# Fourteen seven-product pairs in each half of a down projection, and the group tiles of the up projection joined

## The chip, the cores and the metric

The kernel runs on one core of a Trainium2 chip. A core has a matrix engine (TensorE, PE in the profile, with its weight loads as PEld), a vector engine (VectorE, DVE), an activation engine (ScalarE, ACT), a general one (GpSimd, POOL), a queue for transfers (SyncE, SP), and 16 DMA engines that all queues share. The metric is the device time of one execution in microseconds; lower is better.

## The reference, cut to what matters

One layer of an encoder on 256 positions (`T`) of width 2048. The change lies in the last part, the channel mixer, whose middle width is 5504 (43 chunks of 128):

```python
def conv_ffn(x, g_norm, w_up, conv_k, conv_b, w_down):
    h = rms_norm(x, g_norm)
    up = h @ w_up                                    # 2048 -> 2 * 5504
    t = up.shape[1]
    pad = jnp.pad(up, ((0, 0), (1, 1), (0, 0)))
    up = (pad[:, :t] * conv_k[0] + pad[:, 1:t + 1] * conv_k[1]
          + pad[:, 2:t + 2] * conv_k[2] + conv_b)
    gate, val = jnp.split(up, 2, axis=-1)
    return x + (jax.nn.silu(gate) * val) @ w_down    # 5504 -> 2048
```

Before it stand a mixer block (`x @ w_in`, a gated branch, neighbourhood attention, two merging projections), after it a final RMS norm. All data is float32.

## The kernel before, in words

**Precision.** Each matrix operand is split into a high part (ScalarE copies it into a tile of a shorter float type) and a low part (VectorE subtracts that from the original). A block product is three matmuls: high by high, low by high, high by low (`triple`, lines 317 to 319).

**Pieces.** Weights come in pieces of 512 KB or less. `load_to` starts the load of a piece on SP's queue (line 145 or 151) into one of five tiles `wraw`; `split_to` makes its high part `whi` (ScalarE, line 170) and its low part `wlo` (VectorE, line 171), each in one of four tiles, so that a piece's part can be written once TensorE has read that of the piece four before. `begin(i)` runs at each piece `i`: it loads up to five pieces ahead, splits up to three ahead, then runs the tasks that were hung on step `i` with `at(i, f)`. The order in which the program calls the operations is the order on every engine; nothing is reordered later. So an operation that waits holds back all that stands behind it on its engine.

**Up projection** (`run_group`, `spread_products`, lines 222 and 226). There are 22 groups of eight pieces. A group makes two chunks of the gate and two of the value (the last group, chunk 42, one of each). Its products with the low weights come in one go for two pieces. When a group's products are done, `ev_up(f0, nb)` takes the results out of PSUM: a ScalarE copy (`tb`) and a VectorE sum (`ta`) for each chunk. Then, as tasks on the steps of the next group, `conv(b)` multiplies by the norm's factor (line 1067), ScalarE makes the middle tap (line 1069), VectorE adds the side taps (lines 1072 and 1074); `gate` follows one step later, and the split of the result into `ff["a"]` one more. The two chunks of a group are done in turn: `conv(0)` one step after the group, `conv(1)` three steps after it, or five for the group before the last. 256 columns each.

**Seven products instead of eight.** The down projection works in two halves of 1024 output columns, each a run of 43 pieces (one chunk of 128 rows each). For two row blocks of positions and two column blocks of 512, a pair of pieces takes 2 x 12 matmuls, or, in the places listed in `DOWN_QUADS`, 21 (Strassen's scheme in Winograd's form, `run_wide`). Such a pair needs sums of its activations and sums of its weights. The sums of activations are made once in the up projection, written to memory by POOL's queue (`ff["kept"]`, line 1094) and read back for each half (`stored`, line 1391). The sums of weights are made on VectorE from the loaded pieces (`weight_sums`, `weight_sums_split`), except for the pairs in `DOWN_SPLIT`: their sums and splits are made during the up projection by `split_ahead` (lines 1286 to 1301), written to memory, and read back as four tiles of 512 KB (`split_read`, line 1251); such a pair then loads half of its first piece. The kept tiles are single ones (`h13`, `l13`, `h24`, `l24` in the pool `twice`), the kept activation sums go round three tiles.

**Places.** Before, each half has 13 such pairs, four of them kept (6, 10, 14, 18), and the first half's first is the fourth pair. `DOWN_JOBS` names the groups of the up projection in which the jobs of `split_ahead` run, one for each kept pair and half.

Lines in the profile are those of the kernel file. The functions that the change touches:

Of the kernel before, what the change touches and what calls it, by code (L numbers as in the profile page):

```python
# [8 lines left out]
F32 = mybir.dt.float32  # L9
BF16 = mybir.dt.bfloat16  # L10
F32R = mybir.dt.float32r
AF = mybir.ActivationFunctionType
# [4 lines left out]
T = 256  # L17
# [50 lines left out]
TURN_X2 = (13, 1)  # L68
Y_GAP = 224
PAD = 16  # L70
DOWN_PAIRS = (3, 5, 6, 7, 9, 10, 11, 13, 14, 15, 17, 18, 19)
DOWN_QUADS = (DOWN_PAIRS, (2, 4, 5, 6, 8, 9, 10, 12, 13, 14, 16, 17, 18))
DOWN_SPLIT = (6, 10, 14, 18)
DOWN_JOBS = ((1, 3), (5, 7), (9, 11), (13, 17))
FIN_AT = 36


# [1 line left out]
def trunk_kernel(ctx, tc, x, x_t, vecs, w_in, ln_g, ln_b, w_st, b_s, rpb, w_branch, w_out, w_up, w_down,  # L79
# [4 lines left out]
    def pool(name, side="left", bufs=1, space=None):  # L84
        kw = {} if space is None else {"space": space}
        st = ExitStack()
        p = st.enter_context(tc.tile_pool(name=name, bufs=bufs, side=side, reuse_waits="tile", **kw))
        return p, st
# [100 lines left out]
    def at(i, f):  # L189
        tasks.setdefault(i, []).append(f)  # L190
# [130 lines left out]
    def act_blocks(w, a11, a21, a12, a22):  # L321
        s3, n1, p2, s4 = (w[:, n * 128:(n + 1) * 128] for n in range(4))
        nc.vector.tensor_sub(s3, a11, a21)
        nc.vector.tensor_sub(n1, a22, a21)
        nc.vector.tensor_add(p2, n1, a11)
        nc.vector.tensor_sub(s4, a12, p2)
# [213 lines left out]
    def split_plain(p, dst):  # L540
        nc.scalar.activation(dst[:, 0, :], p, AF.Copy)
        nc.vector.tensor_sub(dst[:, 1, :], p, dst[:, 0, :].bitcast(F32))
# [508 lines left out]

    def ev_up(f0, nb):
        def done(ps, i):
            n = nb
            a = []
            own = {}
            for p in ps:
                t = turns["p"].tile([128, T], F32, name="tb", bufs=3)
                nc.scalar.activation(t, p[:, T:], AF.Copy)
                u = turns["p"].tile([128, T], F32, name="ta", bufs=6)  # L1060
                nc.vector.tensor_add(u, p[:, :T], t)
                a.append(u)

            def conv(b):
                c = []
                for u, ch in ((a[b], f0 + b), (a[n + b], NF + f0 + b)):
                    nc.vector.tensor_mul(u, u, rs["rb"])  # L1067
                    v = ff["p"].tile([128, T], F32, name="tc", bufs=4)
                    nc.scalar.activation(v, u, AF.Identity, scale=ck[:, 1, ch:ch + 1], bias=ck[:, 3, ch:ch + 1])  # L1069
                    c.append((u, v, ch))  # L1070
                for u, v, ch in c:
                    nc.vector.scalar_tensor_tensor(v[:, 1:], u[:, :T - 1], ck[:, 0, ch:ch + 1], v[:, 1:],  # L1072
                                                   op0=OP.mult, op1=OP.add)
                    nc.vector.scalar_tensor_tensor(v[:, :T - 1], u[:, 1:], ck[:, 2, ch:ch + 1], v[:, :T - 1],
                                                   op0=OP.mult, op1=OP.add)
                at(cur[0] + 1, lambda: gate(b, c[0][1], c[1][1]))

            def gate(b, g, v):
                nc.scalar.activation(g, g, AF.Silu)
                nc.vector.tensor_mul(g, g, v)  # L1080
                at(cur[0] + 1, lambda: split_plain(g, ff["a"][f0 + b]))
                own[b] = g
                if b and f0 // 2 in ff["kept"]:
                    at(cur[0] + 2, sums)
                    at(cur[0] + 3, sums_split)

            def sums():
                own["w"] = ff["more"].tile([128, 512], F32, name="sw")
                act_blocks(own["w"], *(own[k][:, t * 128:(t + 1) * 128] for k in range(2) for t in range(2)))

            def sums_split():
                o = ff["more"].tile([128, 2, 512], F32R, name="so")
                split_plain(own["w"], o)
                nc.gpsimd.dma_start(ff["kept"][f0 // 2], o.bitcast(F32))

            at(i + 1, lambda: conv(0))
            if n > 1:
                at(i + (5 if f0 + 3 == NF else 3), lambda: conv(1))
        return done


# [297 lines left out]
    def down_order(g):  # L1399
# [4 lines left out]

    g_dn = [wide(w_d, 0, down_order(g), g * 1024, lambda k: ff["a"][k], DOWN_QUADS[g], down_room,
                 (ev_sums(2 * g, down_room), ev_down if g == 0 else finish), stored=stored,
                 split=({p: (6, 6) for p in DOWN_SPLIT}, split_read(d_kept, g, down_split_tile))) for g in range(2)]
    ff["kept"] = {p: dram.tile([128, 2, 512], F32, name=f"sums{p}") for p in DOWN_PAIRS}
    for p, turn in zip(DOWN_SPLIT, DOWN_JOBS):
        for g in range(2):  # L1410
# [101 lines left out]
    ctx.push(fa_st)  # L1512
    ff["ap"] = [fa.tile([128, min(2, NF - k), 2, T], F32R, name=f"a{k // 2}") for k in range(0, NF, 2)]
    ff["a"] = [ff["ap"][k // 2][:, k % 2] for k in range(NF)]
    turns["p"], turns_st = pool("turns2")
    ff["more"], more_st = pool("more")
    fc = {}

# [1 line left out]
        ff["p"], fc["st"] = pool("conv", "right")  # L1520

    at(g_up[0][1] + 3, open_conv)
    for g in g_up:
        run_group(g)
    def open_twice():
        more_st.close()
        turns_st.close()
        ff["twice"], twice_st = pool("twice")
        ctx.push(twice_st)

    at(g_dn[0][1] + 3, open_twice)

    def open_fin():
        fc["st"].close()
# [56 lines left out]
```

## Time and profile before

| | |
|---|---|
| median of 3 runs | 1292.68 us (1291.73 to 1294.64) |
| the profiled execution | 1291.66 us |
| its span (first to last instruction) | 1289.9 us |
| busy: TensorE, VectorE, ScalarE, GpSimd | 1279.3, 1120.4, 795.5, 169.0 us |
| moved by DMA | 369.51 MB, 286 GB/s over the span |
| TensorE's granted clock | 0.998 of full speed |

Busy time is the union of an engine's instructions. Matmuls overlap and their ends are modelled, so starts are the safer reading there. A row of a timeline gives start, duration and engine of an instruction or of a run of equal ones (x4), and in brackets how long the engine stood idle before it and what ended that.

### The profile page before, as it was taken

Reading aid. Unit: us, or ns where it says so; the run is one execution under the profiler, and the core shown is the slowest. Engines: PE = TensorE matmul, PEld = TensorE weight load, DVE = VectorE, ACT = ScalarE, POOL = GpSimd, SP = SyncE. Lnnn points to the kernel's source line nnn. Section 1 sums busy time; section 2 is a strip of 40 time slices with the busy share of each in tenths; the row PEclk is TensorE's granted clock in tenths of the full one; section 3 lists DMA queues with packets and bytes.
Section 4 is the critical chain, followed back from the end, with each engine's and each line's share of the span. In section 5 each row is a group of like instructions: output and inputs, shape, how many; then the busy total and the mean of one; then the engine's idle time right before and its main releaser. Section 6 shows DMA issues by size and latency. Waiting matters only on the chain.

```text
span 1289.9 us, 19698 instructions
## 1 busy us (share of the span) xinstructions
PE 1279.3 (99%) x6717; PEld 1088.6 (84%) x6717; DVE 1120.4 (87%) x1664; ACT 795.5 (62%) x1181; POOL 169.0 (13%) x307
## 2 busy tenths in 40 slices
PE   9999999999999999999999999999999999999997
PEld 7888888888887888888888888888888888888885
DVE  7898977777789988996889899898988989889987
ACT  7766566766655655566565666566665656655654
POOL 0003706513000001100001001100000001211210
PEclk9999999999999999999999999999999999999999
DMA  9779889899789977965588788888866859998993
GB/s 367 275 277 277 279 273 340 292 325 321 258 309 345 350 240 254 401 222 169 185 290 280 238 291 294 268 270 285 266 221 220 280 171 357 373 390 319 361 384 141
DMA packets 199893, 369.51 MB, mean 286 GB/s; under 512 B 15984, under 2 KB 124144, under 8 KB 199792
## 3 DMA queue, kind: packets, MB, share of 16 engines
q1 hardware_dynamic: 175472, 286.36, 64.8%
q0 software_dynamic: 23888, 81.23, 17.8%
q8 instruction: 52, 0.85, 0.3%
q10 hardware_dynamic: 432, 0.66, 0.1%
q14 instruction: 49, 0.40, 0.1%
HBM read 320.48 MB, written 45.61 MB: 284 GB/s over the span
## 4 chain that ended last, share of the span: by engine, by line
PE 96%; DVE 2%; DMA 1%; issue 1%; DVEq 0%; ACT 0%; SPq 0%; ACTq 0%
PE bank L222 31%; PE bank L226 16%; PE bank L319 11%; PE bank L317 11%; PE bank L318 11%; PE bank L250 5%; PE bank L252 5%; PE bank L251 5%; DVE wlo L171 1%; DMA wraw<-in_w_down_dram 1%; PE bank L867 0%; PE bank L819 0%; PE bank L857 0%; DMA xr<-in_x_t_dram 0%; PE bank L698 0%
## 5 line engine op out<-in xcount | busy, mean ns | idle before, releaser
L171 DVE TENSOR_TENSOR wlo<-wraw,whi 128x1024 fp32r<-128x1024 f32 (+1 forms) x472 | 537.8, 1152 | 124.4 <-ACT whi L170 76.8
L170 ACT ACTIVATE whi<-wraw 128x1024 fp32r<-128x1024 f32 (+1 forms) x472 | 463.6, 995 | 227.1 <-PE bank L318 65.2
L222 PE MATMUL bank<-h,whi 128*128 128x512 f32 x1760 | 423.6, 391 | 0.0
L222 PEld LDWEIGHTS bank<-h,whi 128*128 128x128 f32 x1760 | 322.7, 188 | 62.6 <-issue 0.5
L226 PEld LDWEIGHTS bank<-h,wlo 128*128 128x128 f32 x1760 | 225.9, 191 | 8.7
L226 PE MATMUL bank<-h,wlo 128*128 128x256 f32 x1760 | 228.6, 283 | 0.0
L1069 ACT ACTIVATE tc<-ta,ck 128x256 f32<-128x256 f32 x86 | 47.1, 595 | 110.0 <-DVE ta L1067 110.0
L319 PE MATMUL bank<-wlo,a 128*128 128x512 f32 x188 | 73.4, 390 | 0.2 <-DVE wlo L171 0.2
L317 PE MATMUL bank<-whi,a 128*128 128x512 f32 x188 | 73.2, 389 | 0.0
L318 PE MATMUL bank<-whi,a 128*128 128x512 f32 x188 | 73.2, 389 | 0.0
L319 PE MATMUL bank<-wlo,h 128*128 128x512 f32 x186 | 72.5, 390 | 0.1
L318 PE MATMUL bank<-whi,h 128*128 128x512 f32 x186 | 72.5, 390 | 0.0
L317 PE MATMUL bank<-whi,h 128*128 128x512 f32 x186 | 72.5, 390 | 0.0
L1072 DVE SCALAR_TENSOR_TENSOR tc<-ta,ck,tc 128x255 f32<-128x255 f32 x86 | 41.4, 482 | 14.4 <-ACT tc L1069 14.4
L250 PE MATMUL bank<-whi,y 128*128 128x512 f32 x128 | 50.4, 394 | 0.0
L250 PE MATMUL bank<-whi,h 128*128 128x512 f32 x128 | 50.3, 393 | 0.0
L252 PE MATMUL bank<-wlo,y 128*128 128x512 f32 x128 | 49.8, 389 | 0.0
L252 PE MATMUL bank<-wlo,h 128*128 128x512 f32 x128 | 49.8, 389 | 0.0
L251 PE MATMUL bank<-whi,y 128*128 128x512 f32 x128 | 49.8, 389 | 0.0
L251 PE MATMUL bank<-whi,h 128*128 128x512 f32 x128 | 49.8, 389 | 0.0
L1301 POOL DMA_DIRECT2D down_h<-so x16 | 8.7, 545 | 309.3 <-ACT so L1296 187.2
L374 ACT ACTIVATE h<-h 128x1024 fp32r<-128x1024 f32 x36 | 38.0, 1058 | 13.8 <-DVE h L364 7.1
(324 smaller groups left out, 2005.3 us busy)
## 6 DMA issues: line engine op xcount, KB each, us to landing
wraw<-in_w_up_dram SPq DMA_DIRECT2D x336, 256.0 KB, 4.1
wraw<-in_w_in_dram SPq DMA_DIRECT2D x107, 512.0 KB, 6.6
wraw<-in_w_down_dram SPq DMA_DIRECT2D x78, 512.0 KB, 7.2
wraw<-in_w_in_dram SPq DMA_DIRECT2D x70, 256.0 KB, 4.8
wraw<-in_w_branch_dram SPq DMA_DIRECT2D x32, 512.0 KB, 5.5
wraw<-in_w_out_dram SPq DMA_DIRECT2D x28, 512.0 KB, 5.9
h<-sums POOLq DMA_DIRECT2D x18, 512.0 KB, 7.5
tw<-in_w_down_dram POOLq DMA_DIRECT2D x8, 1024.0 KB, 8.6
```

The lines of the kernel that those rows point to most:

```text
L170: nc.scalar.activation(h[:, k, :m], w[:, k, :m], AF.Copy)
L171: nc.vector.tensor_sub(l[:, k, :m], w[:, k, :m], h[:, k, :m].bitcast(F32))
L222: nc.tensor.matmul(p, h[:, k - k0, b * 128:(b + 1) * 128], acts(k), start=k == 0, stop=k == nk - 1)
L226: nc.tensor.matmul(p[:, :T], l[:, k - k0, b * 128:(b + 1) * 128], acts(k)[:, 0, :], start=False, stop=False)
L250: nc.tensor.matmul(p, xh, h[:, kk, :m], start=st, stop=False)
L251: nc.tensor.matmul(p, xl, h[:, kk, :m], start=False, stop=False)
L252: nc.tensor.matmul(p, xh, l[:, kk, :m], start=False, stop=sp)
L317: nc.tensor.matmul(p, xh, h, start=st, stop=False, **kw)
L318: nc.tensor.matmul(p, xl, h, start=False, stop=False, **kw)
L319: nc.tensor.matmul(p, xh, l, start=False, stop=sp, **kw)
L1069: nc.scalar.activation(v, u, AF.Identity, scale=ck[:, 1, ch:ch + 1], bias=ck[:, 3, ch:ch + 1])
L1072: nc.vector.scalar_tensor_tensor(v[:, 1:], u[:, :T - 1], ck[:, 0, ch:ch + 1], v[:, 1:], op0=OP.mult, op1=OP.add)
```

## The change

Both halves get a fourteenth seven-product pair (pair 2; in the first half it is the third pair in order, in the second half the second), which is also a fifth kept pair. For the first half its kept weights are read six steps ahead and its kept activation sums three. The jobs of the kept pairs run in groups 1, 3, 5 and so on to 19. `ev_up` holds the chunks of a group in one tile for the sums (`ta`) and one for the convolution (`tc`), with one operation where an operation can take the whole tile, and hangs its seven parts on seven steps one after another; this holds for every group, the one before the last too. The kept sums get a tile of their own (`sp`). The pool of the kept tiles is opened three steps before the down projection instead of three steps into it.

```diff
-DOWN_PAIRS = (3, 5, 6, 7, 9, 10, 11, 13, 14, 15, 17, 18, 19)
-DOWN_QUADS = (DOWN_PAIRS, (2, 4, 5, 6, 8, 9, 10, 12, 13, 14, 16, 17, 18))
-DOWN_SPLIT = (6, 10, 14, 18)
-DOWN_JOBS = ((1, 3), (5, 7), (9, 11), (13, 17))
+DOWN_PAIRS = (2, 3, 5, 6, 7, 9, 10, 11, 13, 14, 15, 17, 18, 19)
+DOWN_QUADS = (DOWN_PAIRS, (1, 2, 4, 5, 6, 8, 9, 10, 12, 13, 14, 16, 17, 18))
+DOWN_SPLIT = (2, 6, 10, 14, 18)
+DOWN_JOBS = ((1, 3), (5, 7), (9, 11), (13, 15), (17, 19))
+DOWN_LEADS = ({2: (3, 6, 6)}, {})
...
-            at(i + 1, lambda: conv(0))
-            if n > 1:
-                at(i + (5 if f0 + 3 == NF else 3), lambda: conv(1))
+            u = ff["p"].tile([128, 2 * nb, T], F32, name="ta", bufs=1)
+            for n, p in enumerate(ps):
+                nc.scalar.activation(u[:, n], p[:, T:], AF.Copy)
+                nc.vector.tensor_add(u[:, n], p[:, :T], u[:, n])
+            box = {}
+            channels = [f + b for f in (f0, NF + f0) for b in range(nb)]
+
+            def scale():
+                rb = rs["rb"]
+                nc.vector.tensor_mul(u, u, bass.AP(tensor=rb.tensor, offset=rb.offset,
+                                                   ap=[rb.ap[0], [0, 2 * nb], [1, T]]))
+
+            def middle():
+                v = box["v"] = ff["p"].tile([128, 2 * nb, T], F32, name="tc", bufs=1)
+                for n, ch in enumerate(channels):
+                    nc.scalar.activation(v[:, n], u[:, n], AF.Identity, scale=ck[:, 1, ch:ch + 1],
+                                         bias=ck[:, 3, ch:ch + 1])
+
+            def sides():
+                v = box["v"]
+                for tap, to, of in ((0, slice(1, T), slice(0, T - 1)), (2, slice(0, T - 1), slice(1, T))):
+                    for n, ch in enumerate(channels):
+                        nc.vector.scalar_tensor_tensor(v[:, n, to], u[:, n, of], ck[:, tap, ch:ch + 1], v[:, n, to],
+                                                       op0=OP.mult, op1=OP.add)
+
+            def silu():
+                v = box["v"]
+                nc.scalar.activation(v[:, :nb], v[:, :nb], AF.Silu)
+
+            def gate():
+                v = box["v"]
+                nc.vector.tensor_mul(v[:, :nb], v[:, :nb], v[:, nb:])
+
+            def high():
+                nc.scalar.activation(ff["ap"][f0 // 2][:, :, 0, :], box["v"][:, :nb], AF.Copy)
+
+            def low():
+                v, a = box["v"], ff["ap"][f0 // 2]
+                nc.vector.tensor_sub(a[:, :, 1, :], v[:, :nb], a[:, :, 0, :].bitcast(F32))
+                if f0 // 2 in ff["kept"]:
+                    box["w"] = ff["more"].tile([128, 512], F32, name="sw")
+                    act_blocks(box["w"], *(v[:, k, t * 128:(t + 1) * 128] for k in range(2) for t in range(2)))
+
+            def sums_high():
+                box["o"] = ff["more"].tile([128, 2, 512], F32R, name="sp")
+                nc.scalar.activation(box["o"][:, 0], box["w"], AF.Copy)
+
+            def sums_low():
+                o = box["o"]
+                nc.vector.tensor_sub(o[:, 1], box["w"], o[:, 0].bitcast(F32))
                 nc.gpsimd.dma_start(ff["kept"][f0 // 2], o.bitcast(F32))
 
+            steps = [scale, middle, sides, silu, gate, high, low]
+            if f0 // 2 in ff["kept"]:
+                steps += [sums_high, sums_low]
+            for n, step in enumerate(steps):
+                at(i + 1 + n, step)
...
-                 split=({p: (6, 6) for p in DOWN_SPLIT}, split_read(d_kept, g, down_split_tile))) for g in range(2)]
+                 split=({p: DOWN_LEADS[g].get(p, (6, 6)) for p in DOWN_SPLIT}, split_read(d_kept, g, down_split_tile))) for g in range(2)]
...
+    def open_twice():
+        more_st.close()
+        ff["twice"], twice_st = pool("twice")
+        ctx.push(twice_st)
+
+    at(g_dn[0][1] - 3, open_twice)
+
     for g in g_up:
         run_group(g)
...
-    at(g_dn[0][1] + 3, open_twice)
```

## Rows read from the trace of the kernel before

**Rows 1.** The page: busy time by engine, and the chain of waits by engine.

```profile
PE 1279.3 (99%) x6717; PEld 1088.6 (84%) x6717; DVE 1120.4 (87%) x1664; ACT 795.5 (62%) x1181; POOL 169.0 (13%) x307
...
PE 96%; DVE 2%; DMA 1%; issue 1%; DVEq 0%; ACT 0%; SPq 0%; ACTq 0%
```

**Rows 2.** Busy time by stretch: up groups, last up group, first down half.

```profile
core 0: us, PE busy (x) PEld busy (x) DVE busy (x) ACT busy (x) POOL busy (x), PEclk, DMA share, GB/s
588.40:1053.60 465.20, 465.20 (x2685) 411.46 (x2685) 410.73 (x696) 286.55 (x453) 28.74 (x51) 1.00 0.77 251
1053.60:1064.70 11.10, 11.10 (x65) 9.79 (x64) 9.66 (x20) 6.75 (x14) 0.99 (x2) 1.00 0.81 242
1064.70:1172.90 108.20, 108.20 (x478) 89.34 (x477) 98.88 (x123) 63.27 (x74) 19.63 (x38) 1.00 1.00 378
```

**Rows 3.** Timeline of TensorE in the first down half.

```profile
1070.39 0.39 PE L317 MATMUL bank<-whi,a 128*128 128x512 f32 x1
...
1092.60 0.39 PE L319 MATMUL bank<-wlo,a 128*128 128x512 f32 x1
```

**Rows 4.** Groups by line and shape, up projection: busy us, mean ns, idle before.

```profile
L171 DVE TENSOR_TENSOR wlo<-wraw,whi 128x1024 fp32r<-128x1024 f32 x157 | 191.2, 1222 | 28.5 <-ACT whi L170 11.4 <-issue 7.7 <-PE bank L226 6.5
L170 ACT ACTIVATE whi<-wraw 128x1024 fp32r<-128x1024 f32 x156 | 161.7, 1049 | 7.1 <-PE bank L222 6.6
L1069 ACT ACTIVATE tc<-ta,ck 128x256 f32<-128x256 f32 x80 | 43.8, 595 | 104.7 <-DVE ta L1067 104.7
L1072 DVE SCALAR_TENSOR_TENSOR tc<-ta,ck,tc 128x255 f32<-128x255 f32 x80 | 38.5, 482 | 13.4 <-ACT tc L1069 13.4
L1067 DVE TENSOR_TENSOR ta<-ta,rb 128x256 f32<-128x256 f32 x80 | 30.2, 419 | 0.0
```

**Rows 5.** Timeline of VectorE around the last up group.

```profile
1052.53 0.69 DVE L542 TENSOR_TENSOR so<-sw,so 128x512 fp32r<-128x512 f32 x1
...
1056.10 0.69 DVE L171 TENSOR_TENSOR wlo<-wraw,whi 128x512 fp32r<-128x512 f32 x1 [0.48 <-PE bank L226]
1056.71 0.75 DVE L1067 TENSOR_TENSOR ta<-ta,rb 128x256 f32<-128x256 f32 x2
...
1058.32 0.48 DVE L1074 SCALAR_TENSOR_TENSOR tc<-ta,ck,tc 128x255 f32<-128x255 f32 x1
1058.72 0.48 DVE L1072 SCALAR_TENSOR_TENSOR tc<-ta,ck,tc 128x255 f32<-128x255 f32 x1
...
1061.66 0.69 DVE L171 TENSOR_TENSOR wlo<-wraw,whi 128x512 fp32r<-128x512 f32 x1
...
1063.76 0.75 DVE L1067 TENSOR_TENSOR ta<-ta,rb 128x256 f32<-128x256 f32 x2
```

**Rows 6.** Timeline of TensorE around the last up group.

```profile
1055.37 1.11 PE L226 MATMUL bank<-h,wlo 128*128 128x256 f32 x8
...
1063.77 0.64 PE L226 MATMUL bank<-h,wlo 128*128 128x256 f32 x4
...
1065.18 0.39 PE L319 MATMUL bank<-wlo,a 128*128 128x512 f32 x1
```

**Rows 7.** Timeline of ScalarE in the last up group.

```profile
1057.16 1.09 ACT L1069 ACTIVATE tc<-ta,ck 128x256 f32<-128x256 f32 x2 [1.75 <-DVE ta L1067]
1058.16 0.62 ACT L170 ACTIVATE whi<-wraw 128x512 fp32r<-128x512 f32 x1
```

**Rows 8.** DMA issues by tile: count, KB each, median us to landing.

```profile
h<-down_h POOLq DMA_DIRECT2D x16, 512.0 KB, 9.2
```

**Rows 9.** DMA by stretch: the seam, the change of halves, the second half.

```profile
1056.00:1068.00 12.00, 12.00 (x68) 10.19 (x66) 10.76 (x21) 7.75 (x13) 1.07 (x2) 1.00 0.83 235
...
1173.00:1206.00 33.00, 33.00 (x148) 27.32 (x147) 31.69 (x40) 20.49 (x28) 4.71 (x9) 1.00 0.81 275
1206.00:1260.00 54.00, 54.00 (x240) 44.74 (x239) 46.45 (x57) 30.44 (x35) 7.97 (x16) 1.00 1.01 394
```

**Rows 10.** The chain that ended last, near the end of the down projection.

```profile
1247.39 11.36 DMA wraw<-in_w_down_dram
...
1271.90 1.23 DVE wlo L171
```

More of the change, by code (lines that the diff above doesn't have):

```diff
@@ L1053, in done @@
         def done(ps, i):
[L1054 to L1089, printed above, removed]
@@ L1091, in sums_split @@
-            def sums_split():
-                o = ff["more"].tile([128, 2, 512], F32R, name="so")
-                split_plain(own["w"], o)
-                nc.gpsimd.dma_start(ff["kept"][f0 // 2], o.bitcast(F32))
-            at(i + 1, lambda: conv(0))
-            if n > 1:
-                at(i + (5 if f0 + 3 == NF else 3), lambda: conv(1))
+            u = ff["p"].tile([128, 2 * nb, T], F32, name="ta", bufs=1)
+            for n, p in enumerate(ps):
+                nc.scalar.activation(u[:, n], p[:, T:], AF.Copy)
+                nc.vector.tensor_add(u[:, n], p[:, :T], u[:, n])
@@ L1514, in trunk_kernel @@
     ff["a"] = [ff["ap"][k // 2][:, k % 2] for k in range(NF)]
-    turns["p"], turns_st = pool("turns2")
     ff["more"], more_st = pool("more")
@@ L1522, in trunk_kernel @@
     at(g_up[0][1] + 3, open_conv)
+    def open_twice():
[3 more added lines that the diff above has]
+    at(g_dn[0][1] - 3, open_twice)
     for g in g_up:
         run_group(g)
[L1525 to L1529, printed above, removed]
-    at(g_dn[0][1] + 3, open_twice)
     def open_fin():
```

## The prediction, made before the changed kernel was run

> **What bounds the kernel now.** I read the page first: its table of engines and its chain of waits [rows 1]. TensorE is busy for 99% of the span and carries 96% of the chain, VectorE (DVE) is busy for 87%. A share over the whole span hides the stages, so I then asked for each engine's busy time by stretch [rows 2]: the up projection to its last group but one, that last group alone, and the first half of the down projection. In all three TensorE shows no idle time (465.20 of 465.20, 11.10 of 11.10, 108.20 of 108.20 us). So TensorE's instruction stream sets the time there, and two things can move it: fewer products, or a product that has to wait. The same rows say which neighbours are close to being late: in the first down half the DMA engines' share is 1.00 at 378 GB/s and VectorE is at 98.88 of 108.20 us.
>
> The busy time of one product is modelled, so its price is taken from starts. In the timeline of TensorE the product that starts at 1070.39 and the one at 1092.60 have 98 steps between them, all 128x512 [rows 3]: 22.21 / 98 = 0.2266 us each.
>
> The tight place is the seam between the two stages. The last up group has one column block of each kind, so its eight pieces (U1 to U8 below; D0 is the first piece of the down projection) take 11.10 us, 1.39 each, where each of the 21 groups before it takes 465.20 / 21 = 22.2 us, 2.8 a piece. VectorE does 9.66 us of work in those 11.10 [rows 2].
>
> **Removed products.** A half has 43 pieces of 12 products less three for each seven-product pair: 516 - 39 = 477 before (the row of the first half counts 478, one of them on the edge [rows 2]) and 516 - 42 = 474 after. Two halves lose 6 products, 6 x 0.2266 = 1.36 us, all on the path. Gain: 1.36 us.
>
> **The joined tiles inside the up projection.** Four multiplications of 256 columns at 419 ns become one of 1024 columns, for which the nearest row is a 128x1024 subtraction at 1222 ns [rows 4]; two pairs of 256-column operations become two of 512 columns at about 0.69 [rows 5]. A group costs VectorE 1.68 + 0.84 + 0.84 = 3.36 us for these before and 1.22 + 0.69 + 0.69 = 2.60 after; 21 groups give back 16 us. Against that stand the fifth kept pair, twice (four 512-column sums and two 1024-column splits, 4 x 0.69 + 2 x 1.22 = 5.2 us each), and one more set of kept activation sums, four operations of 128 columns (each under the 419 ns of 256) and one of 512, at most 2.4 us: 12.8 us. VectorE falls by some 3 us of 410.73 and TensorE, always busy there, does not notice: 0 on the path. If that cover were gone the bounds are a loss or gain of the whole 3 us; I take 0, because in a full group a step lasts 2.8 us and the weights are split three steps ahead. Each added DMA of these jobs goes to POOL's queue, where only other kept data stands behind it.
>
> **The seam, step by step.** This is where joining costs. A step first splits the piece three ahead (ScalarE makes the high part, VectorE the low part), then runs its tasks. Before, the group of pair 20 did one half of its convolution at U2 and the other as late as U6: VectorE starts it at 1056.71, and the second multiplication at 1063.76, after D0's split. The low part of U8 is started at 1061.66 and ready by 1062.35 [rows 5], and TensorE's products with it start at 1063.77 [rows 6]: 1.4 us to spare. After, the second half of the convolution is no longer put off; scale, middle, sides, silu, gate stand at U2, U3, U4, U5, U6, and a convolution of four channels lies ahead of U8's split. In order:
>
> - VectorE's low part of U5 waits for TensorE's low products of U1, which start at 1055.37 [rows 6], so it still starts at 1056.10, and the next instruction 0.61 later, at 1056.71 [rows 5]. Nothing upstream can move this earlier.
> - At U2 two things follow: the low part of pair 19's kept sums (512 columns, before done at 1052.53, ahead of this stretch [rows 5]), 0.61; and the joined scale, 1.22 less the 0.08 by which neighbours overlap: 1058.46.
> - At U3 ScalarE runs the four middle taps. Two take 1.09 [rows 7], four 2.18: until about 1060.7. In before only two ran here.
> - U7's high part stands behind them on ScalarE, 0.62 [rows 7]: 1061.3. U7's low part stands behind that on VectorE, 0.61: 1061.9. VectorE sits idle for over 2 us for it.
> - At U4 the eight side taps. Independent ones start 0.40 apart (1058.32 to 1058.72 [rows 5]): 3.2 us, until 1065.15. U8's low part stands behind them, 0.69: 1065.85.
>
> TensorE wants it at 1063.77, so it waits 2.1 us. Queued behind that wait are the rest of the low products, the last high product and D0. D0's high part on ScalarE now stands behind silu (six of the eight taps must be done, 1064.4; 0.62 for silu, priced like the high part of equal size [rows 7], 1.05 for D0's part [rows 4]: 1066.1), its low part ends at about 1067.4, and TensorE, moved by 2.1 from 1065.18 [rows 6], wants it at 1067.3: 0.1 more. With full durations in place of overlapped ones (0.69, 1.22, four middle taps at 0.595, 0.62, 0.69, eight side taps at 0.482, 0.69 [rows 4, 5, 7]) the same sum ends at 1066.9, a wait of 3.2 us. Bounds 0 (should the order be kinder than I read it) and 3.2; I take 2.2, since the overlapped steps are rows of this very stretch. Behind the seam VectorE has less to do than before (the postponed convolution that starts at 1063.76 is gone), so nothing further is late.
>
> **The added transfers.** A kept pair replaces 256 KB of weights by four tiles of 512 KB [rows 8], plus 512 KB of kept sums: 2304 KB or 2.36 MB in each half, 4.72 MB. The reads are ordered on POOL ahead of the following kept pairs; the wait for the single set of kept-weight tiles moves the reads of pair 6 back, in each half, to the end of pair 2's products. At 394 GB/s, the rate of the saturated stretch, 4.72 MB take 12.0 us. The shares leave idle (1 - 0.83) x 12 = 2.0 us at the seam and (1 - 0.81) x 33 = 6.3 us after the change of halves [rows 9], which are just where pair 2 is read. 12.0 - 8.3 = 3.7 us are not covered by idle time and come out of the lead that loads have. How thin the lead gets is told by the chain near the end: a weight load takes 11.36 us, and from its landing on VectorE's work runs without a gap into the low part that starts at 1271.90 and that the chain runs through [rows 10]. Bounds: 0 (lead holds) to 3.7 us; I take 0, because the seam's wait gives the queues 2.2 us more in the first half and the idle 6.3 us cover the second.
>
> Here a rule of the Trainium skill speaks against the change: "DMA: Bandwidth & Descriptors", section "Where 436 GB/s comes from", puts the limit for transfers between HBM and SBUF at about 358 GB/s for a core. The trace shows 378 GB/s over 108 us and 394 over 54 us, so it does not bind here at that figure.
>
> **Sum.** The profiled execution took 1291.66 us, of which 1289.9 are span. 1291.66 - 1.36 + 2.2 = 1292.5. The median of the runs, 1292.68, lies 1.02 above the profiled one, so the forecast is 1293.5, given as 1293.4. Differences within 0.2% (2.6 us) cannot be told from none, and this is one of those.
>
> **Rivals.**
> - A, the sum above: 1292.6 to 1294.6 with the seam at 1.3 to 3.2 us. Chance 0.55.
> - B, the seam costs nothing: some other engine's progress frees the order, and only the products count. 1292.68 - 1.36 = 1291.3. For it speaks that VectorE's total falls; against it the idle time that ScalarE's four middle taps force on VectorE. Chance 0.25.
> - C, slower: the down projection becomes bound by its transfers. Place: the saturated stretches; price: the uncovered 3.7 us, less whatever lead is left, on top of the seam. With half of it 1295.4, with all 1297.2. It decides once the uncovered transfer time exceeds the lead. Against it: in before the first half's products waited for nothing through 108 us at a share of 1.00 [rows 2]. Chance 0.14. If instead 358 GB/s were a ceiling, the first half's 378 x 108.2 = 40.9 MB and 2.4 added would need 121 us in place of 107.5, and the time would be about 1306; the rows give that 0.01. That ceiling is the skill's, named above.
> - D, the four copies into one joined tile wait for each other's sums (each sum must end before the next copy starts): three sums of about 0.42 [rows 4] then lie between the first copy and the last, the seam starts some 1.3 us later and its wait grows by as much: about 1294.8. Chance 0.05.
>
> **Chances and range.** A is within 0.2% almost whole, B too but for a few hundredths, C and a part of D are slower: faster 0.04, same 0.78, slower 0.18. The range reaches from B's 1291.3 less the scatter of the runs to the middle of C: 1290.7 to 1296.0.
>
> **What would show it.** Right: 948 products between the seam and the end; a gap of about 2 us in TensorE's products near 1064, released by VectorE's low part; before that gap VectorE idle behind ScalarE's middle taps; the stretch from 588 to 1053 unchanged in length; kept reads of pair 2 landing before their products. Wrong: no gap at the seam (B), or products in the down projection that wait for weights, kept tiles or sums, with a DMA share of 1 through the change of halves (C). A shift inside the full up groups would refute the price of zero there.

## The result, and the profile after

The changed kernel takes 1296.7 us (median of 11 runs, 1295.6 to 1302.46), the kernel before 1292.48 beside it: a ratio of 1.0041, with a 95% interval of 1.0033 to 1.0050 (it is worked out from all runs; the quotient of the two medians is 1.0033). So it is slower by more than 0.2%, where 1293.4 and no difference were forecast; 1296.7 is also above the range, which ended at 1296.0. Of the eleven runs the four with a mean granted clock of 0.999 took 1295.6 to 1296.94 us, and the three at 0.996 or below 1300.3 to 1302.46.

The page of after, for [rows 1]: busy time by engine, and the chain by engine.

```profile
PE 1279.2 (99%) x6711; PEld 1088.0 (84%) x6711; DVE 1111.5 (86%) x1575; ACT 794.8 (61%) x1144; POOL 179.9 (14%) x328
...
PE 95%; DMA 2%; DVE 2%; issue 0%; ACT 0%; POOL 0%; SPq 0%; DVEq 0%; ACTq 0%
```

Six products fewer, VectorE lighter by 9 us, and yet a longer span (1293.8 for 1289.9). The totals only say that something waits. Here is after by stretch, for [rows 2] and [rows 9]; columns as there:

```profile
588.40:1053.60 465.20, 465.20 (x2685) 411.48 (x2684) 401.56 (x607) 286.71 (x417) 34.90 (x62) 1.00 0.80 264
1053.60:1064.70 11.10, 11.10 (x63) 9.56 (x61) 8.90 (x20) 6.41 (x14) 2.10 (x4) 1.00 0.83 265
1064.70:1172.90 108.20, 104.64 (x460) 85.56 (x460) 95.23 (x117) 61.86 (x72) 21.03 (x40) 1.00 0.97 383
...
1173.00:1206.00 33.00, 33.00 (x147) 27.31 (x147) 31.30 (x43) 18.22 (x26) 4.76 (x9) 1.00 0.94 358
```

The up projection is untouched (465.20 of 465.20, with 2685 products as before). TensorE loses its time in the third row, 3.56 us. Its timeline has three gaps there, in brackets with what ended them:

```profile
1066.63 0.74 PE L227 MATMUL bank<-h,wlo 128*128 128x256 f32 x4 [1.85 <-DVE wlo L172]
...
1085.42 0.50 PE L320 MATMUL bank<-wlo,a 128*128 128x512 f32 x1 [0.61 <-DVE wlo L172]
...
1104.50 0.50 PE L320 MATMUL bank<-l,h 128*128 128x512 f32 x1 [1.11 <-DMA l<-down_l]
```

**The first gap** is the forecast one. VectorE and ScalarE around it, for [rows 5] and [rows 7]:

```profile
1058.18 1.22 DVE L1064 TENSOR_TENSOR ta<-ta,rb 128x1024 f32<-128x1024 f32 x1
1059.32 0.68 DVE L172 TENSOR_TENSOR wlo<-wraw,whi 128x512 fp32r<-128x512 f32 x1
1062.13 0.69 DVE L172 TENSOR_TENSOR wlo<-wraw,whi 128x512 fp32r<-128x512 f32 x1 [2.13 <-ACT whi L171]
1062.74 3.24 DVE L1077 SCALAR_TENSOR_TENSOR tc<-ta,ck,tc 128x255 f32<-128x255 f32 x8
1065.90 0.68 DVE L172 TENSOR_TENSOR wlo<-wraw,whi 128x512 fp32r<-128x512 f32 x1
```

```profile
1059.50 2.08 ACT L1070 ACTIVATE tc<-ta,ck 128x256 f32<-128x256 f32 x4 [2.30 <-DVE ta L1064]
```

Four middle taps on ScalarE (2.08 for 2.18 forecast), VectorE idle for 2.13 us behind them, eight side taps in 3.24 for 3.2, and only then the low part of U8.

**The second gap** is 0.77 us longer than the usual step between products. VectorE a little later:

```profile
1080.63 0.69 DVE L365 TENSOR_TENSOR h<-wraw 128x512 f32<-128x512 f32 x1 [0.42 <-DMA wraw<-in_w_down_dram]
...
1082.57 1.66 DVE L1077 SCALAR_TENSOR_TENSOR tc<-ta,ck,tc 128x255 f32<-128x255 f32 x4
1084.15 1.22 DVE L172 TENSOR_TENSOR wlo<-wraw,whi 128x1024 fp32r<-128x1024 f32 x1
```

The low part that TensorE wants stands behind four side taps: those of the last up group (chunk 42), which nothing needs for another 90 us. In before they start at 1073.64, ahead of pair 3's weight sums (1077.56 to 1080); as steps of their own they come two pieces later and fall behind these sums, which wait for a transfer.

**The third gap**, 1.27 us, ends with a read. POOL's queue:

```profile
1064.97 0.53 POOL L1264 DMA_DIRECT2D l<-down_l  x1 [4.06 <-DMA sums<-sp]
1065.49 0.53 POOL L1404 DMA_DIRECT2D h<-sums  x1
1068.13 0.53 POOL L1404 DMA_DIRECT2D h<-sums  x1 [2.12 <-PE bank L223]
...
1088.96 0.53 POOL L1404 DMA_DIRECT2D h<-sums  x1 [19.78 <-PE bank L320]
...
1091.04 0.53 POOL L1264 DMA_DIRECT2D l<-down_l  x1
```

The read at 1088.96 is that of pair 6's sums; its four kept weight tiles stand behind it, the last issued at 1091.04 and landed 13.42 us later. In the chain that ended last it reads:

```profile
1091.04 13.42 DMA l<-down_l
```

The read at 1088.96 waits for a tile that pair 3 holds until its products end. In `wide`, `for n, lead in zip(("13", "24"), ready[-2:])` leaves 6 in `lead`, so each plain pair after the first kept pair reads its sums six pieces ahead, not four. With pair 2 the first kept pair, pair 3's sums come ahead of pair 2's own, take the tile h6, and pair 6, which takes h6 next, gets it one pair later than if pair 2 had held it.

The profiles, in us (starts of products; the seam is the last 50 products ahead of D0; the second half ends with the start of its last product; "late at the last split" is what one step near 1273 to 1278 us takes beyond 0.227, where a product waits for a low part; "four edits" is the version at the end of the experiments):

| | before, 4 profiles | after, 2 profiles | four edits, 2 profiles |
|---|---|---|---|
| seam | 8.63 to 8.64 | 10.73, 10.74 | 8.64, 8.64 |
| first half | 108.31 to 108.57 | 110.14, 110.85 | 107.71, 107.98 |
| second half | 108.34 to 108.68 | 107.21, 108.65 | 107.66, 108.76 |
| last product to end | 8.40 to 8.42 | 8.80, 8.74 | 8.43, 8.39 |
| late at the last split | 0.32 to 0.63 | 0, 1.26 | 0.30, 1.35 |

### The profile page after: what moved, and what is told of

Read it like the earlier page. It is cut to its first block, busy times and chain, and to the rows that moved or that the text cites. A ratio compares the mean times of both kernels' runs of the same rounds, so it can differ in the third digit from the quotient of the medians.

```text
span 1293.8 us, 19640 instructions
## 1 busy us (share of the span) xinstructions
PE 1279.2 (99%) x6711; PEld 1088.0 (84%) x6711; DVE 1111.5 (86%) x1575; ACT 794.8 (61%) x1144; POOL 179.9 (14%) x328
## 4 chain that ended last, share of the span: by engine, by line
PE 95%; DMA 2%; DVE 2%; issue 0%; ACT 0%; POOL 0%; SPq 0%; DVEq 0%; ACTq 0%
PE bank L223 31%; PE bank L227 16%; PE bank L320 11%; PE bank L318 11%; PE bank L319 11%; PE bank L251 5%; PE bank L253 4%; PE bank L252 4%; DMA l<-down_l 1%; DMA wraw<-in_w_in_dram 1%; DVE wlo L172 1%; PE bank L868 0%; PE bank L820 0%; PE bank L858 0%; PE bank L499 0%
## 5 line engine op out<-in xcount | busy, mean ns | idle before, releaser
L1077 DVE SCALAR_TENSOR_TENSOR tc<-ta,ck,tc 128x255 f32<-128x255 f32 x172 | 69.8, 479 | 0.0
L320 PE MATMUL bank<-wlo,a 128*128 128x512 f32 x176 | 68.7, 390 | 0.6 <-DVE wlo L172 0.6
L319 PE MATMUL bank<-whi,a 128*128 128x512 f32 x176 | 68.5, 389 | 0.0
L318 PE MATMUL bank<-whi,a 128*128 128x512 f32 x176 | 68.5, 389 | 0.0
L1304 DVE TENSOR_TENSOR tw<-tw 128x512 f32<-128x512 f32 x72 | 50.3, 699 | 0.7
L786 POOL TENSOR_SCALAR_AFFINE_SELECT bias<-run 64x128 f32<-64x128 f32 x64 | 35.5, 588 | 80.8 <-DVE sc L828 80.2
```

The source lines that it names most:

```text
L318: nc.tensor.matmul(p, xh, h, start=st, stop=False, **kw)
L319: nc.tensor.matmul(p, xl, h, start=False, stop=False, **kw)
L320: nc.tensor.matmul(p, xh, l, start=False, stop=sp, **kw)
L1077: nc.vector.scalar_tensor_tensor(v[:, n, to], u[:, n, of], ck[:, tap, ch:ch + 1], v[:, n, to], op0=OP.mult, op1=OP.add)
L1304: nc.vector.tensor_add(w[:, d], w[:, a], w[:, b])
```

## The experiments

Ratios are to before on the same chip, with 95% intervals. The traces are one profile each; waits of a product are given from the start of the product before it, as time beyond the usual step.

**1. The joined tiles alone.** Pairs, jobs and pool order of before.

```diff
-DOWN_PAIRS = (2, 3, 5, 6, 7, 9, 10, 11, 13, 14, 15, 17, 18, 19)
...
-DOWN_SPLIT = (2, 6, 10, 14, 18)
...
+DOWN_PAIRS = (3, 5, 6, 7, 9, 10, 11, 13, 14, 15, 17, 18, 19)
...
+DOWN_SPLIT = (6, 10, 14, 18)
...
-    at(g_dn[0][1] - 3, open_twice)
+    at(g_dn[0][1] + 3, open_twice)
```

> The kernel after with the thirteen pairs, the four jobs and the pool order of the kernel before: only the joined group tiles of the up projection are left of the change. Theory (the joined steps of pair 20's group stand ahead of the last pieces' splits at the seam): the first down product starts 2.1 us later than before, nothing else moves, so about 1294.6 us, 2.1 over the kernel before. Rival (the late seam comes from the kept reads and the writes that the fifth kept pair adds): without them the seam is as before, about 1292.5 us.

1295.78 us, 1.0027 (1.0017 to 1.0036). The seam takes 10.73 us without any added transfer, so the first gap is the joining's. But that is over a microsecond dearer than forecast. Windows of this kernel behind the gap, columns as in [rows 2]:

```profile
1068.00:1070.00 2.00, 2.00 (x6) 1.61 (x6) 1.64 (x2) 1.46 (x2) 2.00 (x4) 0.50 0.66 188
1070.00:1072.00 2.00, 2.00 (x8) 1.58 (x7) 1.84 (x3) 1.61 (x4) 1.06 (x3) 0.68 1.01 205
1072.00:1074.00 2.00, 2.00 (x11) 1.62 (x10) 2.00 (x4) 1.06 (x1) 0.00 (x0) 1.00 0.95 369
```

After TensorE had been idle for 1.85 us, it ran for some 3.4 us at 0.50, the lower of its two clocks (1.2 GHz): 6 products in 2 us where there are 10 or 11. In after's first profile the same gap was followed by 1.00.

**2. The seam alone.** Pair 20's steps three pieces later, behind the last splits of the up projection.

```diff
-                at(i + 1 + n, step)
+                at(i + (4 if f0 + 3 == NF else 1) + n, step)
```

> The kernel after, with all seven steps of pair 20's group three pieces later, so that the last two pieces of the up projection are split ahead of its long middle and sides. Theory: the 2.09 us at the seam go, the two waits in the first half stay (0.77 and 1.27), so about 1294.6 us. Rival (the steps now stand ahead of the first down pieces' splits, or the reads of the kept sums bound the start of the half anyway): what the seam gives is lost again within the first eight down pieces, 1296.3 to 1297.0 us.

1297.96 us, 1.0051 (1.0038 to 1.0065): no gain on after, whose interval overlaps. The seam is back at 8.64 us, as the theory said, but the first half takes 113.50: TensorE, now earlier, waits 2.84 us at 1076.78 for the sums of pair 2, then runs at the lower clock, and at 1103.4 waits 1.27 for pair 6's kept tiles. So the theory is refuted. The rival had the loss and one of its causes, the reads of the kept sums, and still put the time too low (1296.3 to 1297.0).

**3. The order of the reads alone.** Pair 2's sums a piece earlier, ahead of pair 3's.

```diff
-DOWN_LEADS = ({2: (3, 6, 6)}, {})
+DOWN_LEADS = ({2: (4, 6, 6)}, {})
```

> The kernel after, with the sums of pair 2 read one piece earlier, which puts them ahead of those of pair 3 on GpSimd's queue and gives them the tile that pair 6 takes next. Theory (pair 6's reads are late because the tile they queue behind comes free only after pair 3's products): the reads of pair 6 are issued about 5 us earlier, the wait of 1.27 us near 1103 us goes, about 1295.4 us. Rival (the added transfers are too slow wherever they stand): the wait moves or shrinks by under 0.4 us, 1296.3 to 1296.7 us.

1295.48 us, 1.0032 (1.0019 to 1.0044). In its trace no product waits at the place of the third gap. The median is 1.2 us below after's, as forecast, but the intervals overlap, so the times alone do not show the gain.

**4. Both.**

> The two edits together (the steps of pair 20's group three pieces later, the sums of pair 2 read ahead of those of pair 3). Theory: both gains add, 1296.7 - 2.1 - 1.3 = 1293.3 us, of which the wait for the eighth down piece (0.77) is still a part. Rival (the same transfers bound the start of the first half whichever queue order they have): under 1 us of gain, 1295.7 us or more.

1294.68 us, 1.0022 (1.0013 to 1.0030): 2.0 of the 3.4 us that the sum promised. What is left in the trace: 0.67 at 1077.8 for pair 2's sums, and 1.66 at 1083.1, the second gap, twice its size in after. In the second half it waits 0.97 at 1198 and 1.06 at the last split.

**5. Joined tiles with the seam's edit (1 and 2).**

> The kernel with only the joined tiles (thirteen pairs), with the steps of pair 20's group three pieces later. Theory (the joining costs at the seam alone: the late splits, and the slower clock that the idle TensorE is granted after them): TensorE is never idle by a microsecond there, the clock stays at 1.00, and the time is the kernel before's, 1291.8 to 1292.8 us. Rival (the joined steps are dear wherever they stand, because one step is twice as long): 1294 us or more.

1294.05 us, 1.0014 (1.0005 to 1.0023). The seam takes 8.63, the clock stays at 1.00, and one gap of 1.57 us is left, at 1082.1: the second gap, in a kernel without the added transfers. TensorE's waits from 1050 to 1110 us in this run (idle us in total, times, longest):

```profile
PE bank L320 <- DVE wlo L172: 1.4, 1, 1.4
```

Neither theory had it. The rival's time (1294 or more) came out, but its cause, a step twice as long, is refuted by run 10.

**6. The reads of pairs 3 and 5 two pieces later**, on top of run 4, as in before.

```diff
-                for n, lead in zip(("13", "24"), ready[-2:]):
-                    at(i - lead, lambda b=b, k=k, n=n: split[1](k // 2, b, n))
+                for n, early in zip(("13", "24"), ready[-2:]):
+                    at(i - early, lambda b=b, k=k, n=n: split[1](k // 2, b, n))
+                lead = lead if len(ready) == 3 and src is w_d else early
```

> The kernel with both edits of the run before (seam and order of pair 2's sums), and the sums of pairs 3 and 5 read two pieces later, four pieces ahead of their use as in the kernel before. Theory (from 1060 to 1090 us the transfers are the bound, at 405 to 424 GB/s with all queues busy, so what is read early for pairs 3 and 5 delays the pieces and sums of pair 2 that are due first): the waits at 1077.8 us (0.66) and 1083.1 us (1.66) shrink by about 1.2 us together, 1293.5 us. Rival (the waits are those of VectorE's queue, not of bytes): no change, 1294.3 to 1295.0 us.

1295.53 us, 1.0029 (1.0018 to 1.0041): a miss. In its trace the wait at 1077.8 is down to 0.31, but the one at 1083 grew to 2.0 and the clock fell behind it, as it did behind one of 2.2 at the last split. (This profile is the slowest of its six runs, 1298.37 us.)

**7. Half the bytes in pair 2's kept reads**, on top of run 4, with the same instructions. This kernel leaves out half of that pair's weight sums and uses the other half twice, so it is for timing alone.

```diff
+                half = slice(0, 1 if (pair, g) == (2, 0) and kept is d_kept else 2)
-                queue.dma_start(t.bitcast(F32), src)
+                queue.dma_start(t.bitcast(F32)[:, half], src[:, half])
...
+                    box["t"].update({3: box["t"][1], 2: box["t"][4]})
```

> The kernel with both edits (seam and order of pair 2's sums), in which the four kept reads of pair 2 in the first half take 256 KB each instead of 512 KB, with the same instructions in the same order (two of the four weight sums of that pair are used twice in place of the others). Theory (bytes bound the start of the half): 1.05 MB less at some 410 GB/s is 2.6 us, so all that lands behind them is up to 2.5 us earlier; the wait for pair 2's sums at 1077.8 us (0.66) goes and the one at 1083.1 us falls to what the last group's sides on VectorE's queue leave of it (0.3 to 0.8): 1293.0 to 1293.6 us. Rival (order and number of the transfers decide, not their bytes): 1294.4 to 1295.0 us.

1295.14 us, 1.0020 (1.0011 to 1.0029): a miss in time. The wait at 1077.8 is gone, and the second gap again took it up (2.44 us, the lower clock behind it). The three profiles of runs 5 to 7 agree: whatever brings TensorE there sooner is lost to VectorE's queue.

**8. The last group's steps twelve pieces later**, on top of run 6.

```diff
-                at(i + (4 if f0 + 3 == NF else 1) + n, step)
+                at(i + {NF - 3: 4, NF - 1: 13}.get(f0, 1) + n, step)
```

> The kernel of the run with the later sums of pairs 3 and 5, and in addition the last group's scale, middle, sides and what follows twelve pieces later, where no split of a due piece is queued behind them. Theory: what is left of the wait at 1083.1 us goes (its split stood behind 1.66 us of sides on VectorE's queue): 1292.5 to 1293.2 us. Rival (that split waits for its transfer anyway): equal to the run without this edit within 0.3 us.

1291.94 us, 0.9998 (0.9990 to 1.0007). No wait over 0.12 us is left in the first half, which takes 107.71 us. Window of this kernel over the place of the second gap:

```profile
1072.00:1084.00 12.00, 12.00 (x54) 9.65 (x53) 10.76 (x14) 6.38 (x8) 2.62 (x5) 1.00 1.03 418
```

The transfers run at 418 GB/s, their engines busy throughout, and TensorE is busy for 12.00 of 12.00. In run 6, without this one edit, it was busy for 10.54 of these 12 us. So the second gap is one of queue order.

**9. The same edit of the last group, alone on after.**

> The kernel after, with nothing changed but the last group's steps (scale, middle, sides and what follows), which come twelve pieces later. Theory (the wait of 0.77 us at 1084.4 is that of a split queued behind those sides on VectorE): this wait goes, the 2.1 us at the seam and the 1.27 near 1103 us stay, about 1295.9 us. Rival (that split waits for its transfer): no change, 1296.4 to 1297.0 us.

1299.96 us, 1.0054 (1.0041 to 1.0066): the highest median of all, with an interval that overlaps after's. The second gap is gone, but pair 6's kept tiles, issued at the same moment as in after (1089.0 to 1091.1), now come 3.8 us late in three waits from 1101.7 to 1107.3, with the lower clock behind. The last lands 16.15 us after its issue, in after 13.42. The loads of the pieces, which the second gap had held back, are issued 0.6 to 1.0 us sooner among those reads; that this makes the 2.7 us is argued and not tested.

**10. Joined tiles with both edits of the steps, thirteen pairs.**

> Thirteen pairs with the joined tiles, the steps of pair 20's group three pieces later and the last group's twelve later. Theory (the joined steps cost only by what they stand ahead of at the seam and in the first pieces of the down projection): no wait over 0.3 us between 1060 and 1100 us, the first half takes 108.4 us as in the kernel before, the time is that of before within 0.5 us, 1291.9 to 1292.7 us. Rival (joining has another price): 1293.3 us or more, half of the first half's excess left.

1292.41 us, 1.0001 (0.9992 to 1.0010). Within the interval, joining costs nothing when its steps stand elsewhere.

**11. Run 8 with pairs 3 and 5 read six pieces ahead.**

> Fourteen pairs with the steps of pair 20's group three pieces later, the last group's twelve later, and pair 2's sums ahead of those of pair 3, but the sums of pairs 3 and 5 read six pieces ahead again. Theory (VectorE's queue was the larger wait, the bytes the smaller): the wait at 1083 us is gone, that at 1077.8 us (0.66) is back or moved, 1292.3 to 1292.9 us. Rival (the later reads of pairs 3 and 5 are what freed the start of the half): 1293.5 us or more.

1292.32 us, 0.9998 (0.9990 to 1.0007); one gap of 0.9 us at 1077.5 for pair 2's sums, as the theory said. So the later reads of pairs 3 and 5 are not needed for the time.

**12. Both edits of the steps, reads as in after.**

> Fourteen pairs with both edits of the steps (pair 20's group three pieces later, the last group's twelve), and all reads as in the kernel after. Theory (the order of the reads is a cost of its own): the wait for pair 2's sums near 1076.8 us (2.85) and the one for pair 6's kept reads near 1103 us (1.27) are there, with a slower clock behind the first, 1295.5 to 1297.0 us. Rival (only the steps matter): 1292 to 1293 us.

1298.12 us, 1.0041 (1.0027 to 1.0055). With the steps cured, the reads alone cost: 3.4 us of waiting for pair 2's sums at 1077.3, issued at 1068.21 behind pair 3's and landed at 1080.88, the lower clock behind it, and 0.35 at 1104.6. The chain that leads to the late product, from the trace of this run:

```profile
1058.50 8.14 DMA sums<-sp
1066.64 0.53 issue
1067.17 0.53 POOL l L1264
1067.70 0.51 POOL h L1404
1068.21 12.67 DMA h<-sums
```

It begins with the write of pair 19's sums. POOL's queue stands 6.57 us (in after 4.06) at pair 2's fourth kept tile; the profile puts this down to that write, and the code opens the pool of the kept tiles as it closes the one with those sums. Both reads of sums stand behind it. In before the write was issued at 1053.76, ahead of any such read:

```profile
1053.76 0.53 POOL L1094 DMA_DIRECT2D sums<-so  x1 [21.45 <-DVE so L542]
```

How much of the 3.4 us an earlier write or a later pool would give back, no run here tests.

**13. Run 12 with half the bytes in pair 2's kept reads**, as in 7 (half of its weight sums left out).

> The kernel with both edits of the steps and all reads in the order of the kernel after, in which the four kept reads of pair 2 in the first half take 256 KB each instead of 512 KB (two of that pair's four weight sums are used twice in place of the others). Theory (bytes: at 417 to 420 GB/s 1.05 MB are 2.5 us): pair 2's sums land about 2.5 us earlier, the wait for them falls from 3.4 to about 0.9 us and no slower clock follows it, 1.5 to 2.5 us less overall than the run with whole reads, 1295.6 to 1296.6 us. Rival (the sums are late by their place in the queue alone): the wait stays above 2.5 us and the time at 1297.5 us or more.

1296.39 us, 1.0036 (1.0023 to 1.0049), an interval that overlaps run 12's. In the trace pair 2's sums, issued at 1068.38, land at 1076.66, and no product waits for them: at that place bytes ahead count (the 1.05 MB left out explain 2.5 of the 4.4 us by which the transfer is shorter; the rest I can't place). But pair 6's tiles, still issued behind pair 3's products, are then 4.0 us late.

**14 to 16. Before, three more profiles**, the first timed against itself.

> The kernel before, unchanged, profiled and timed against itself. Theory (what after lost ahead of the changed code is how executions differ): this second profile reaches the group of the up projection at which the first one stood at 1053.78 us up to 1 us later, with the same 8.64 us at the seam and 108.4 us in each half; ratio 1.000 within 0.001. Rival: it is there at 1053.8 us again within 0.1.

> The kernel before, unchanged, a third profile. If the late start of the changed stages is how executions differ, the product that stood at 1053.78 and 1054.07 us in the first two lies between 1053.6 and 1055.4 us; if the change causes it, below 1054.2 us again.

> The kernel before, unchanged, a fourth profile, as the third: above 1054.2 us in at least one of the two if executions differ so, below in both if the change causes the late start.

1292.41 us (1.0003, 0.9994 to 1.0012), 1292.19 and 1292.46. The product of the up projection that stood at 1053.78 us stands at 1054.07, 1054.16 and 1054.52. In after it stood at 1054.64, in its second profile at 1053.29: what after's first profile lost ahead of the change, 0.86, is how executions differ.

**17. The version of run 8 once more.**

> The version with all four edits (both edits of the steps, both of the reads) once more, timed. If the six products are all that is left of the change, 1290.6 to 1291.4 us where before takes 1292.2, a ratio of 0.9989; if something ahead of the changed stages gives 0.7 us back, 1291.6 to 1292.0 us. Its halves take 107.7 us each, as in its first profile.

1291.75 us, 0.9999 (0.9990 to 1.0008). Its first half takes 107.98, its second 108.76, and there the gain went: the last split stands on VectorE behind five sums of the last pair, 1.35 us too late, where the first profile of this version lost 0.30. VectorE there:

```profile
1268.64 0.68 DVE L991 TENSOR_TENSOR x<-bank,x 128x512 f32<-128x512 f32 x1
...
1271.88 1.22 DVE L172 TENSOR_TENSOR wlo<-wraw,whi 128x1024 fp32r<-128x1024 f32 x1
```

**18. After once more.**

> The kernel after, unchanged, a second profile. If the clock is at risk after the seam's wait in this kernel too, this profile or its time shows either 1295.6 to 1297 us with the clock at 1.00 behind the seam, or some 1.6 us and more above that with stretches at 0.50 behind one of its waits.

1296.35 us. The clock fell in this kernel too, behind the same gap:

```profile
1065.29 0.74 PE L227 MATMUL bank<-h,wlo 128*128 128x256 f32 x4 [1.85 <-DVE wlo L172]
...
1067.13 0.63 PE L320 MATMUL bank<-wlo,a 128*128 128x512 f32 x1
1067.56 0.63 PE L318 MATMUL bank<-whi,a 128*128 128x512 f32 x1
1067.99 0.63 PE L319 MATMUL bank<-whi,a 128*128 128x512 f32 x1
```

Starts lie 0.43 us apart where [rows 3] have 0.227: the nine steps from 1066.33 to 1069.97 take 3.64 us in place of 2.04, 1.6 us more. TensorE came that much later to the place of the second gap and had none there.

## Why the prediction was wrong, by its steps

Against the profiled execution the sum said 1292.5; it took 1295.60, 3.1 more: 0.86 ahead of any changed code, -0.11 at the seam, 2.47 in the first half, -0.50 in the second, 0.37 behind the last product. The -0.50 is luck of that execution, in which nothing waited at the last split; the second profile of after waited 1.26 there. That 1296.7 falls into the band of rival C (1295.4 to 1297.2) is luck too: two of the three gaps of after stand behind VectorE's queue.

- **Removed products: right in size.** In run 8, where products wait 0.12 us in the first half and 0.30 at the last split (0.37 in [rows 2]'s kernel), the halves are 107.71 and 107.66, 0.64 and 0.73 less than [rows 2]'s kernel: 1.37 for 1.36 forecast. The step took them as "all on the path". In the second half that holds only in part: the last split was late by 0.2 to 0.63 us in all seven profiles with thirteen pairs, and by 0 to 2.2 in the thirteen with fourteen, over 1 us in eight of these. TensorE, with three products fewer, comes there sooner and mostly waits longer.
- **Joined tiles inside the up projection: right**, 465.20 before and after. Only VectorE's saving was mis-sized, at no cost: 401.56 for 410.73, 9.2 us in place of 3.
- **The seam: right**, by its own chain of instructions: 2.09 for 2.2. What the step did not have is the clock: in run 1 and run 18 the same gap drew 1.6 to 1.7 us more behind it. Run 1 against run 10 is 3.4 us in the medians; the two differ in both edits of the steps, so that is the price of the seam's gap, the clock and the second gap together.
- **"Behind the seam VectorE has less to do than before ..., so nothing further is late": failed.** It counted pair 20's steps and not the last group's, which were split up by the same edit. Their sides moved from ahead of pair 3's weight sums to behind them, and ahead of the low part that TensorE wants. Run 5 shows this wait without the added transfers (1.57 us), and from 5 to 10 (1294.05 to 1292.41) it goes with one edit.
- **The added transfers at 0: the step that failed most.** It failed at two places of POOL's queue. The text had pair 6's reads moved back "to the end of pair 2's products"; they were moved to the end of pair 3's, since they queue behind a read of sums whose tile pair 3 held: 1.27 us in after, gone in run 3. And pair 2's own sums were to land ahead of their products; they stand behind pair 3's and behind the write of pair 19's sums, which the text did not have on this path: 3.39 us in run 12. The price of the order of the reads, with the steps cured, is run 12 over run 11, which differ in that one edit and ran on the same chip: 5.8 us in the medians, the lower clock included. That "the seam's wait gives the queues 2.2 us more" was true, and it is why after itself does not show it all: the seam's gap hid the late sums of pair 2 (run 2 uncovers them) and, by run 9, the second gap a part of pair 6's. After the change of halves the text was right in that the idle time covered the reads: the share rose from 0.81 to 0.94, and no product of after waits there.
- **Rival C** had the mechanism in part. Its main place was not the saturated end but the first 40 us of the half. From 1060 to 1084 us the rate is 396 GB/s where before moves 343, and how late a read lands there depends on the bytes ahead of it (run 13) as well as on its turn (runs 3 and 11). A higher price than zero needed that stretch, and the sum took the idle share around the seam as room. At the saturated end the longer wait for the last split is a smaller part of it: in run 18 the chain into that split goes over a load of 11.29 us, as the one of [rows 10] over 11.36. C's neighbour with a ceiling of 358 GB/s is refuted: run 8 moves 418 GB/s for 12 us. That figure is the Trainium skill's ("DMA: Bandwidth & Descriptors", "Where 436 GB/s comes from"); the higher one of that section, 435 for the ports of SBUF, is the one the runs come near.
- **Rivals B and D** are refuted: the seam's gap was there, and the four copies and sums of the joined tile took no longer than the forecast chain (2.09).

With all four edits the change is neither faster nor slower than before by what can be measured (0.9998 and 0.9999). That the 1.37 us of the traces are 0.2 in the medians is in part the longer wait at the last split (run 17 shows it for one execution, the thirteen profiles for their kind); the rest is open. Open too is how much of pair 2's wait is due to the write of pair 19's sums. Not explained either: the 0.34 to 0.40 us behind the last product in both profiles of after (and in runs 3 and 9, the other fourteen-pair kernels with the seam's gap), and 0.4 us more around the span in the thirteen-pair joined kernels (2.2 where the others have 1.8).

## What to carry to other kernels

When steps of a group are split up or joined, write out every in-order queue past the boundary until the last of them has run, the last group's among them: a step that nobody needs soon costs as much ahead of a due split as one that is due. A read is issued when the tile at the head of its queue comes free, so follow tiles and not the pairs that they serve, and look for a write that must land first. And waits in a chain hide each other: two of the edits gave nothing when made alone (runs 2 and 9), and with the third (run 11) they brought the kernel back to the time of before.

## What the runs showed of the hardware

- A gap of about 1.85 us in TensorE's products was followed by the full clock in one profile of after and in run 9, and by some 3.4 us at half clock in the other profile of after and in runs 1 and 3. So a wait costs its own length and, in some executions, 1.6 to 1.7 us more.
- At the lower clock the products of 512 columns start 0.426 us apart. The Trainium skill ("TensorE: Matmul & The Clock Gate", "Wait — 56ns, not 53.3ns?") gives 426.7 ns for that clock, which agrees, and 215.7 at the full one, where [rows 3] show 226.6; the account goes by the measured steps.
